# Reading the moving operand of every fp32r product as two interleaved streams, in a two-layer streaming encoder

## The chip, the core and the metric

The kernel runs on one core of one Trainium2 chip. The metric is device time in microseconds for one execution, from the first to the last instruction of the program with what lies around it. A program's time is the median of several executions; the profile is of one more execution, whose span is given beside it.

## The reference

The reference is a trunk of two layers on an input of 1024 frames by 1024 features, in float32. Every layer is `x = x + mixer(RMSNorm(x))`, and a final RMSNorm follows. Layer 0 projects the normalised input to 7168 columns, runs a diagonal complex state-space layer with a GLU on one part and retention over eight heads on another, multiplies each by its own SiLU gate and maps both back. Layer 1 is a gated convolution module. Cut to its matrix products:

```python
def mixer_ab(h, w_in, ...):
    proj = h @ w_in                                   # 1024 x 1024 by 1024 x 7168
    u_s5, g_s5, q, k, v, g_ret = jnp.split(proj, cuts, axis=-1)
    y_s5 = s5_mixer(u_s5, ...)                        # holds gelu(y) * sigmoid(y @ glu_w + glu_b)
    y_s5 = y_s5 * jax.nn.silu(g_s5)
    y_ret = retention(q, k, v) * jax.nn.silu(g_ret)
    return jnp.concatenate([y_s5, y_ret], axis=-1) @ w_out     # 2048 columns to 1024

def mixer_conv(h, w_in, conv_w, conv_b, ln_g, ln_b, w_out):
    a, b, g = jnp.split(h @ w_in, 3, axis=-1)         # 1024 x 1024 by 1024 x 3072
    u = a * jax.nn.sigmoid(b)
    u = causal_depthwise_conv(u, conv_w) + conv_b     # 31 taps
    u = jax.nn.silu(layernorm(u)) * jax.nn.silu(g)
    return u @ w_out                                  # 1024 x 1024 by 1024 x 1024
```

## The kernel before, in words

Activations lie with their features on the 128 partitions and the frames along the free dimension, so that a row block of 128 features by 1024 frames is worked on in two halves of 512 frames (`HALF`). A large matrix product is a loop over output row blocks `nb`, halves `h` and eight blocks `kb` of the contraction.

**How a float32 product is made of fp32r products.** Every float32 operand is split into a high part in the type fp32r and a low part, the rest, in fp32r as well (`xh`, `xl`, `wh`, `wl`). `mm3` (lines 175 to 183) then issues three products into the same PSUM bank: `wh` with `xh` (L181), `wh` with `xl` (L182) and `wl` with `xh` (L183). The weight block of 128 by 128 is stationary and 512 frames of the activations move through it. `gemm` calls `mm3` for eight blocks of the contraction, so one bank takes 24 products. In the value projection of retention the roles are turned: 128 frames are stationary and the weights move, 256 columns at a time in `ret_values` (L1091 to L1093) and 512 in `ret_values_wide` (L1114 to L1116). The last row blocks of the last projection (`mm_oc`) are taken in quarters of 256 frames.

These products are, by the program's names: `mm_u` 384, `mm_g` of layer 0 768, `mm_k` and `mm_q` 192 each, `mm_v` 192 of 512 columns and 384 of 256, `mm_glu` 336, `mm_wo` 768, `mm_b`, `mm_a` and `mm_g` of layer 1 384 each, and `mm_oc` 336 of 512 columns and 96 of 256. Together that is 4320 products of 512 columns and 480 of 256 columns. Everywhere the moving operand is a run of adjacent elements. Other products, of the state-space part and of the retention heads, have 128 columns or fewer in float32 and go through lines of their own (L848, L912, L918, L1170, L1204).

**How a bank is emptied.** The banks of these products rotate over three (`ps_mm`), so a bank is wanted again after two other row blocks. Each is read once by VectorE or ScalarE: `u_block` (L358) multiplies by the normalisation `R` and writes the frames in another order, reading bank and `R` at a step of eight elements; `gate_block` (L373), `project` (L1045), `w_out` (L1394), `ab` (L1445) and `w_out_c` (L1672) are VectorE operations on adjacent elements; `ret_values` (L1094, L1118), the tanh of `ab` (L1432) and the SiLU of `gates` (L1457) are ScalarE operations. The GLU forms its product as seven smaller products with sums between them; its partial sums `gu2` and `gu3` are kept in SBUF, and `gated` (L1314) takes the tanh of a finished sum.

**What sets the order.** Code is recorded in Python with priorities (`self.at`) and explicit constraints (`issue_after`), and a scheduler of the tile framework puts each engine's queue in order at build time. Weights come in through SyncE's DMA queue two blocks ahead (`wnext`), are rounded to the high part by ScalarE (L171, L148) and the low part is formed by VectorE or GpSimd (L172) or read back from HBM.

Of the kernel before, what the change touches and what calls it, by code (L numbers as in the profile page):

```python
# [14 lines left out]
AF = mybir.ActivationFunctionType  # L15
# [20 lines left out]
G0 = 3  # L36

# [15 lines left out]
class Trunk:  # L53
# [121 lines left out]
    def mm3(self, ps, w, kb, x, start, stop, more=False):  # L175

        nc = self.nc
        wh, wl = w
        xh, xl = x
        more = {"skip_group_check": True} if more else {}  # L180
        nc.tensor.matmul(ps, wh[:, kb, :], xh, start=start, stop=False, **more)  # L181
        nc.tensor.matmul(ps, wh[:, kb, :], xl, start=False, stop=False, **more)  # L182
        self.last_mm = nc.tensor.matmul(ps, wl[:, kb, :], xh, start=False, stop=stop, **more)  # L183
# [60 lines left out]
    def layer0_front(self, st):  # L244
# [106 lines left out]
        def u_block(nb):  # L351
            ut = uv.tile([P, 8, P], F32, name=f"ut_{nb}", tag="ut", bufs=2)

            def evac(h, ps):
                r = self.R[:, h * HALF:(h + 1) * HALF]

                with self.tc.issue_after(self.u_evac[0].ins) if nb == 1 else nullcontext():
                    self.u_evac[nb] = nc.vector.tensor_tensor(  # L358
                        ut[:, ::-1, h * 64:(h + 1) * 64], ps[:].rearrange("p (m j) -> p j m", j=8),
                        r.rearrange("p (m j) -> p j m", j=8), op=ALU.mult)  # L360
# [7 lines left out]
        def gate_block(nb, w, dst):  # L368
            gt = uv.tile([P, T], F32, name=f"gt_{nb}", tag="ut", bufs=2)

            def evac(h, ps):
                c = slice(h * HALF, (h + 1) * HALF)
                nc.vector.tensor_tensor(gt[:, c], ps[:], self.R[:, c], op=ALU.mult)  # L373
                nc.scalar.activation(gt[:, c], gt[:, c], AF.Silu)
# [653 lines left out]
    def ret_proj(self, pair):  # L1028
# [9 lines left out]
        def project(nm):  # L1038
            w = self.wnext(f"{nm}{pair}")
            raw = raws[nm] = self.rq.tile([P, T], F32, name=f"{nm}raw_{pair}", tag="raw", bufs=2)  # L1040
            for h in range(2):
# [3 lines left out]
                self.last_raw = nc.vector.tensor_tensor(raw[:, c], ps[:], self.R[:, c], op=ALU.mult)  # L1045
# [32 lines left out]
    def ret_values(self, pair):  # L1078
# [4 lines left out]
        for b in range(8):  # L1083
            ps = self.bank(f"mm_v{pair}_{b}", aux=False)
            h, o = b // 4, (b % 4) * P
            for kb in range(KB):
# [3 lines left out]
                wl = wv[i][1][:].rearrange("p (k a) n -> p k (a n)", a=2)[:, k4, :]  # L1090
                nc.tensor.matmul(ps[:, :256], xh[:, o:o + P], wh, start=kb == 0, stop=False)  # L1091
                nc.tensor.matmul(ps[:, :256], xh[:, o:o + P], wl, start=False, stop=False)
                nc.tensor.matmul(ps[:, :256], xl[:, o:o + P], wh, start=False, stop=kb == KB - 1)  # L1093
            self.last_v = nc.scalar.mul(vt[:, b, :], ps[:, :256], self.Rtok[:, b:b + 1])  # L1094
# [4 lines left out]
    def ret_values_wide(self):  # L1099
# [3 lines left out]
        for h in range(2):  # L1103
            vt = self.rp.tile([P, 4, HALF], F32, name=f"v_0_{h}", tag="v", bufs=2)
            pss = [self.bank(f"mm_v0_{h}_{b}") for b in range(4)]
            for j in range(4):
                wh, wl = (t[:].rearrange("p (k a) n -> p k (a n)", a=4)
                          for t in self.wnext(f"v0_{h}_{j}", 1 if h and j == 3 else 2))
                for b in range(4):
                    o = slice(b * P, (b + 1) * P)  # L1110
                    for k in range(2):
                        kb = 2 * j + k
                        xh, xl = self.xs[h][kb]
                        nc.tensor.matmul(pss[b][:], xh[:, o], wh[:, k, :], start=kb == 0, stop=False)  # L1114
                        nc.tensor.matmul(pss[b][:], xh[:, o], wl[:, k, :], start=False, stop=False)
                        nc.tensor.matmul(pss[b][:], xl[:, o], wh[:, k, :], start=False, stop=kb == KB - 1)  # L1116
            for b in range(4):
                last = nc.scalar.mul(vt[:, b, :], pss[b][:], self.Rtok[:, 4 * h + b:4 * h + b + 1])  # L1118
# [122 lines left out]
    def layer0_back_and_layer1(self, st):  # L1241
# [59 lines left out]
        def gated(nb, h, z):  # L1301
# [11 lines left out]
            with self.tc.issue_after(self.last_rs.ins) if h == nb == 0 else nullcontext():  # L1313
                nc.scalar.activation(z[:], src[:], AF.Tanh, scale=0.5, bias=hgb[:, nb:nb + 1])  # L1314
# [29 lines left out]
        for i, x in ((6, t2), (7, t3), (4, t4)):  # L1344
            for m in range(2):
# [18 lines left out]
        for m in range(2):  # L1364
            pss = [self.bank(f"mm_glu5{2 * m + a}", aux=False) for a in range(2)]
            for i, x in ((5, t1), (3, b22)):
                w = wn()
                for a in range(2):
                    n = 2 * m + a
                    product(pss[a], w, a, x, i == 3)  # L1370
                    if i == 5:
                        z = spare(f"mm_gluz{n}", n)
                        v.tensor_tensor(z[:], u3[n][:], pss[a][:], op=ALU.add)
                        gated(4 + n, 1, z)
# [9 lines left out]
        def w_out(h, nbs):  # L1384
            for nb in nbs:
# [8 lines left out]
                v.tensor_tensor(t[:], ps[:], xt[:], op=ALU.add)  # L1394
# [31 lines left out]
        def ab(h):  # L1426
            for nb in range(8):
# [4 lines left out]
                tanh = nc.scalar.activation(sg[:], pb[:], AF.Tanh, scale=0.5)  # L1432
# [12 lines left out]
                v.scalar_tensor_tensor(u[:, PADW:], sg[:], 1.0, pa[:], op0=ALU.add, op1=ALU.mult)  # L1445
# [4 lines left out]
        def gates(halves, nbs, hold={}):  # L1450
            for nb in nbs:
                wg = self.wnext(f"cg{nb}_{halves[0]}")
                for h in halves:
# [3 lines left out]
                    nc.scalar.activation(sg[:], pg[:], AF.Silu)  # L1457
# [196 lines left out]
        def w_out_c(h, nb, cols, hold=None):  # L1654
# [11 lines left out]
            def part(c):  # L1666
# [4 lines left out]
                with self.tc.issue_after(behind.ins) if behind else nullcontext():  # L1671
                    self.last_add = v.tensor_tensor(t[:, c], ps[:, :n], xt[:, c], op=ALU.add)  # L1672
# [230 lines left out]
```

## Time and profile before

| what | value |
|---|---|
| median of 3 runs | 1178.7 us (1178.5 to 1179.73) |
| the profiled execution, span | 1176.5 us, 17212 instructions |
| TensorE matmuls busy | 1168.5 us, 99% |
| TensorE weight loads busy | 979.8 us, 83% |
| VectorE busy | 844.5 us, 72% |
| ScalarE busy | 489.9 us, 42% |
| GpSimd busy | 655.3 us, 56% |
| mean granted TensorE clock | 0.999 |

The profile is that of one execution. In it PE is TensorE's matmul row, PEld its weight loads, DVE VectorE, ACT ScalarE, POOL GpSimd and SP SyncE. `L358` is line 358 of the kernel. Busy time of PE is not a measure of how full the array is, since matmuls overlap in a pipeline: the recorded duration of a matmul of 512 columns is 389 ns although the next one starts 227 ns later. What a product costs is therefore read from the distance of two starts.

### The profile page before, as it was taken

How to read it: one execution, taken by the hardware profiler on the slowest of the kernel's cores; microseconds unless marked ns; L12 is line 12 of the kernel's file. 1: busy time of each engine (PE TensorE's matmuls, PEld its weight loads, DVE VectorE, ACT ScalarE, POOL GpSimd, SP SyncE). 2: the span in 40 equal slices, each digit the busy share in tenths (PEclk: the TensorE clock that was granted, in tenths of full speed). 3: DMA queues.
4: the chain of work that ended last, by engine and by line, in shares of the span. 5: the costliest groups of instructions: out<-in, count | busy, mean ns of one | idle time of the engine just before them, and what ended most of it. 6: DMA issues, size and time to landing. Idle time of an engine off the chain costs nothing.

```text
span 1176.5 us, 17212 instructions
## 1 busy us (share of the span) xinstructions
PE 1168.5 (99%) x6286; PEld 979.8 (83%) x6286; DVE 844.5 (72%) x1464; ACT 489.9 (42%) x719; POOL 655.3 (56%) x448
## 2 busy tenths in 40 slices
PE   9999999999999999999999999999999999999997
PEld 8888888888888888989888888888888888888787
DVE  7975698777418359586679323599999899999834
ACT  6422223222223231333456324455535676344673
POOL 2059999888235444242673110588534567677663
PEclk9999999999999999999999999999999999999999
DMA  9344355555387666769998977665578654367765
GB/s 349 108 139 137 123 151 192 179 168 174 123 268 270 240 226 205 269 199 351 375 352 282 333 267 249 212 206 206 212 242 287 231 179 170 107 188 259 265 219 180
DMA packets 117637, 261.46 MB, mean 222 GB/s; under 512 B 10672, under 2 KB 42288, under 8 KB 116912
## 3 DMA queue, kind: packets, MB, share of 16 engines
q1 hardware_dynamic: 117552, 260.36, 65.5%
q8 instruction: 49, 0.80, 0.3%
q14 instruction: 36, 0.29, 0.1%
HBM read 181.48 MB, written 74.65 MB: 218 GB/s over the span
## 4 chain that ended last, share of the span: by engine, by line
PE 98%; issue 0%; ACT 0%; POOL 0%; DVE 0%; POOLq 0%; ACTq 0%
PE mm_g L181 8%; PE mm_g L182 7%; PE mm_g L183 7%; PE mm_wo L182 5%; PE mm_wo L183 5%; PE mm_wo L181 5%; PE mm_b L183 2%; PE mm_b L182 2%; PE mm_a L183 2%; PE mm_a L182 2%; PE mm_b L181 2%; PE mm_a L181 2%; PE mm_oc L183 2%; PE mm_u L182 2%; PE mm_oc L181 2%; PE mm_oc L182 2%
## 5 line engine op out<-in xcount | busy, mean ns | idle before, releaser
L1510 DVE SCALAR_TENSOR_TENSOR cv<-u,convw,cv 128x512 f32<-128x512 f32 x398 | 273.2, 751 | 11.0 <-ACT cv L1489 9.1
L1483 POOL TENSOR_TENSOR tp<-tp,tp 128x512 f32<-128x512 f32 x64 | 83.8, 1309 | 36.5 <-ACT tp L1482 35.5
L181 PE MATMUL mm_g<-xh,wh_g 128*128 128x512 f32 x256 | 101.8, 398 | 0.0
L183 PE MATMUL mm_g<-xh,wl_g 128*128 128x512 f32 x256 | 100.1, 391 | 0.0
L182 PE MATMUL mm_g<-xl,wh_g 128*128 128x512 f32 x256 | 100.0, 391 | 0.0
L417 POOL TENSOR_TENSOR s1q<-s1q,s1q 128x512 f32<-128x512 f32 x12 | 17.8, 1480 | 86.0 <-ACT s1q L412 86.0
L1482 ACT ACTIVATE tp<-u,convw 128x512 f32<-128x512 f32 x64 | 45.3, 718 | 34.2 <-POOL tp L1483 34.1
L181 PEld LDWEIGHTS mm_g<-xh,wh_g 128*128 128x128 f32 x256 | 48.0, 188 | 11.7 <-issue 1.2
L373 DVE TENSOR_TENSOR gt<-mm_g,R 128x512 f32<-128x512 f32 x32 | 21.9, 684 | 49.3 <-PE mm_g L183 49.3
L183 PEld LDWEIGHTS mm_g<-xh,wl_g 128*128 128x128 f32 x256 | 48.1, 188 | 10.4
L182 PEld LDWEIGHTS mm_g<-xl,wh_g 128*128 128x128 f32 x256 | 48.1, 188 | 9.9 <-issue 0.4
L172 POOL TENSOR_TENSOR wl_glu<-wf_glu,wh_glu 128x1024 fp32r<-128x1024 f32 x14 | 34.0, 2429 | 33.2 <-ACT wh_glu L171 27.4
L182 PE MATMUL mm_oc<-zl,wh_woc 128*128 128x512 f32 (+1 forms) x144 | 52.5, 365 | 0.0
L183 PE MATMUL mm_oc<-zh,wl_woc 128*128 128x512 f32 (+1 forms) x144 | 52.4, 366 | 0.0
L172 POOL TENSOR_TENSOR wl_v<-wf_v,wh_v 128x1024 fp32r<-128x1024 f32 x12 | 30.7, 2566 | 38.4 <-ACT wh_v L171 38.4
L181 PE MATMUL mm_oc<-zh,wh_woc 128*128 128x512 f32 (+1 forms) x144 | 52.1, 373 | 0.0
L181 PE MATMUL mm_wo<-ysh,wh_wos 128*128 128x512 f32 x128 | 50.2, 392 | 0.0
L181 PE MATMUL mm_g<-h1h,wh_cg 128*128 128x512 f32 x128 | 50.2, 392 | 0.0
L183 PE MATMUL mm_b<-h1h,wl_cb 128*128 128x512 f32 x128 | 49.9, 390 | 0.0
L181 PE MATMUL mm_b<-h1h,wh_cb 128*128 128x512 f32 x128 | 49.8, 389 | 0.0
L182 PE MATMUL mm_b<-h1l,wh_cb 128*128 128x512 f32 x128 | 49.8, 389 | 0.0
L182 PE MATMUL mm_wo<-ysl,wh_wos 128*128 128x512 f32 x128 | 49.8, 389 | 0.0
(526 smaller groups left out, 3650.7 us busy)
## 6 DMA issues: line engine op xcount, KB each, us to landing
wf_g<-w_ab SPq DMA_DIRECT2D x16, 512.0 KB
wf_wos<-w_out SPq DMA_DIRECT2D x16, 512.0 KB
wf_wor<-w_out SPq DMA_DIRECT2D x16, 512.0 KB
wf_cb<-w_c SPq DMA_DIRECT2D x16, 512.0 KB
wf_ca<-w_c SPq DMA_DIRECT2D x16, 512.0 KB
wf_woc<-w_out_c SPq DMA_DIRECT2D x16, 512.0 KB
wf_v<-w_v SPq DMA_DIRECT2D x12, 512.0 KB
wf_cg<-w_c SPq DMA_DIRECT2D x11, 512.0 KB
```

The lines of the kernel that those rows point to most:

```text
L172: self.low_made = lo[i].tensor_tensor(wl[:].rearrange(fl)[:, c], wf[:, c], h.bitcast(F32), op=ALU.subtract)
L181: nc.tensor.matmul(ps, wh[:, kb, :], xh, start=start, stop=False, **more)
L182: nc.tensor.matmul(ps, wh[:, kb, :], xl, start=False, stop=False, **more)
L183: self.last_mm = nc.tensor.matmul(ps, wl[:, kb, :], xh, start=False, stop=stop, **more)
L373: nc.vector.tensor_tensor(gt[:, c], ps[:], self.R[:, c], op=ALU.mult)
L417: nc.gpsimd.tensor_tensor(a, a, sq[:], op=ALU.add)
L1482: nc.scalar.mul(sk[:], u[:, k:k + HALF], cw[:, nb, k:k + 1])
L1483: gp.tensor_tensor(s0[:], s0[:], sk[:], op=ALU.add)
L1510: v.scalar_tensor_tensor(dst[:], *tap, accs_[i][:], op0=ALU.mult, op1=ALU.add)
```

## The change

The moving operand of each of the 4800 products is viewed with its columns in another order. The 512 columns are seen as two halves of 256, and the product takes a column of the first half, then one of the second: 0, 256, 1, 257 and so on (for 256 columns: 0, 128, 1, 129). The array writes its results to the bank in the order in which columns arrive, so the bank holds the frames interleaved. Each reader of a bank now reads it with a step of two elements, the even ones and then the odd ones, and writes them as two runs of adjacent elements, which restores the natural order. The stationary operand and its load stay as they are, and the same values are multiplied and summed.

In `u_block` the step in the bank goes from eight elements to sixteen, and `R` is still read at a step of eight. In the GLU the partial sums stay in the interleaved order of the banks, and only the last step (the tanh in `gated`, or the last sum for row blocks 4 to 7) restores the natural one. Because a bank can't be reordered in place, product 4 of the GLU now goes to a bank of the rotating three and its finished sum to a spare bank (`mm_gluy`), where before both were in the spare one.

No instruction is added, removed or moved by this: every engine's queue holds the same operations in the same order as before, apart from that name.

```diff
+LANES = 2
+def mv(ap):
+    return ap.rearrange("p (a c) -> p c a", a=LANES)
+def un(ap):
+    return ap.rearrange("p (c a) -> p a c", a=LANES)
+def nat(ap):
+    return ap.rearrange("p (a c) -> p a c", a=LANES)
...
@@ mm3
         xh, xl = x
+        xh, xl = mv(xh), mv(xl)
...
@@ u_block
+                o = ut[:, ::-1, h * 64:(h + 1) * 64].rearrange("p j (a m) -> p j a m", a=LANES)
...
-                        ut[:, ::-1, h * 64:(h + 1) * 64], ps[:].rearrange("p (m j) -> p j m", j=8),
-                        r.rearrange("p (m j) -> p j m", j=8), op=ALU.mult)
+                        o, ps[:].rearrange("p (m j a) -> p j a m", j=8, a=LANES),
+                        r.rearrange("p (a m j) -> p j a m", j=8, a=LANES), op=ALU.mult)
@@ gate_block (project, w_out and w_out_c alike)
-                nc.vector.tensor_tensor(gt[:, c], ps[:], self.R[:, c], op=ALU.mult)
+                nc.vector.tensor_tensor(nat(gt[:, c]), un(ps[:]), nat(self.R[:, c]), op=ALU.mult)
@@ ret_values (ret_values_wide alike)
+                wh, wl = mv(wh), mv(wl)
...
-            self.last_v = nc.scalar.mul(vt[:, b, :], ps[:, :256], self.Rtok[:, b:b + 1])
+            self.last_v = nc.scalar.mul(nat(vt[:, b, :]), un(ps[:, :256]), self.Rtok[:, b:b + 1])
@@ the GLU
-                nc.scalar.activation(z[:], src[:], AF.Tanh, scale=0.5, bias=hgb[:, nb:nb + 1])
+                nc.scalar.activation(*((z[:], src[:]) if turned else (nat(z[:]), un(src[:]))), AF.Tanh, scale=0.5,
+                                     bias=hgb[:, nb:nb + 1])
...
-                    ps = spare(f"mm_glu{i}{n}", n) if i == 4 else self.bank(f"mm_glu{i}{n}", aux=False)
+                    ps = self.bank(f"mm_glu{i}{n}", aux=False)
...
-                        v.tensor_tensor(ps[:], u3[n][:], ps[:], op=ALU.subtract)
-                        gated(4 + n, 0, ps)
+                        z = spare(f"mm_gluy{n}", n)
+                        v.tensor_tensor(nat(z[:]), un(u3[n][:]), un(ps[:]), op=ALU.subtract)
+                        gated(4 + n, 0, z, True)
@@ ab and gates
-                tanh = nc.scalar.activation(sg[:], pb[:], AF.Tanh, scale=0.5)
+                tanh = nc.scalar.activation(nat(sg[:]), un(pb[:]), AF.Tanh, scale=0.5)
...
-                v.scalar_tensor_tensor(u[:, PADW:], sg[:], 1.0, pa[:], op0=ALU.add, op1=ALU.mult)
+                v.scalar_tensor_tensor(nat(u[:, PADW:]), nat(sg[:]), 1.0, un(pa[:]), op0=ALU.add, op1=ALU.mult)
```

More of the change, by code (lines that the diff above doesn't have):

```diff
@@ L1044, in project @@
                 self.gemm(ps[:], w, self.xs[h])
[L1045 removed]
+                self.last_raw = nc.vector.tensor_tensor(nat(raw[:, c]), un(ps[:]), nat(self.R[:, c]), op=ALU.mult)
             return self.last_raw
@@ L1113, in ret_values_wide @@
                         xh, xl = self.xs[h][kb]
-                        nc.tensor.matmul(pss[b][:], xh[:, o], wh[:, k, :], start=kb == 0, stop=False)
-                        nc.tensor.matmul(pss[b][:], xh[:, o], wl[:, k, :], start=False, stop=False)
-                        nc.tensor.matmul(pss[b][:], xl[:, o], wh[:, k, :], start=False, stop=kb == KB - 1)
+                        wk, wj = mv(wh[:, k, :]), mv(wl[:, k, :])
+                        nc.tensor.matmul(pss[b][:], xh[:, o], wk, start=kb == 0, stop=False)
+                        nc.tensor.matmul(pss[b][:], xh[:, o], wj, start=False, stop=False)
+                        nc.tensor.matmul(pss[b][:], xl[:, o], wk, start=False, stop=kb == KB - 1)
             for b in range(4):
-                last = nc.scalar.mul(vt[:, b, :], pss[b][:], self.Rtok[:, 4 * h + b:4 * h + b + 1])
+                last = nc.scalar.mul(nat(vt[:, b, :]), un(pss[b][:]), self.Rtok[:, 4 * h + b:4 * h + b + 1])
             res.append(vt)
@@ L1299, in layer0_back_and_layer1, with gated @@
         held = []
-        def gated(nb, h, z):
+        def gated(nb, h, z, turned=False):
             yg = lp.tile([P, HALF], F32, name=f"yg{nb}_{h}", tag="u", bufs=5)
@@ L1372, in layer0_back_and_layer1 @@
                         z = spare(f"mm_gluz{n}", n)
-                        v.tensor_tensor(z[:], u3[n][:], pss[a][:], op=ALU.add)
-                        gated(4 + n, 1, z)
+                        v.tensor_tensor(nat(z[:]), un(u3[n][:]), un(pss[a][:]), op=ALU.add)
+                        gated(4 + n, 1, z, True)
                     else:
@@ L1393, in w_out @@
                 t = lp.tile([P, HALF], F32, name=f"x1_{nb}_{h}", tag="ev", bufs=3)
-                v.tensor_tensor(t[:], ps[:], xt[:], op=ALU.add)
+                v.tensor_tensor(nat(t[:]), un(ps[:]), nat(xt[:]), op=ALU.add)
                 nc.sync.dma_start(self.x1_d[rows(nb), hs(h)], t[:])
@@ L1456, in gates @@
                     sg = lp.tile([P, HALF], F32, name=f"sgg{nb}_{h}", tag="ev", bufs=3)
-                    nc.scalar.activation(sg[:], pg[:], AF.Silu)
+                    nc.scalar.activation(nat(sg[:]), un(pg[:]), AF.Silu)
                     nc.sync.dma_start(self.gs_d[rows(nb), hs(h)], sg[:])
@@ L1671, in part @@
                 with self.tc.issue_after(behind.ins) if behind else nullcontext():
-                    self.last_add = v.tensor_tensor(t[:, c], ps[:, :n], xt[:, c], op=ALU.add)
+                    self.last_add = v.tensor_tensor(nat(t[:, c]), un(ps[:, :n]), nat(xt[:, c]), op=ALU.add)
                 with self.tc.issue_after(self.halved.ins) if h == 0 and nb >= N0 else nullcontext():
```

## The prediction

> **What bounds the kernel now.** I read the head of the page first: its span, the busy times, the granted clock and the chain that ended last.
>
> ```profile
> span 1176.5 us, 17212 instructions
> PE 1168.5 (99%) x6286; PEld 979.8 (83%) x6286; DVE 844.5 (72%) x1464; ACT 489.9 (42%) x719; POOL 655.3 (56%) x448
> ...
> PEclk9999999999999999999999999999999999999999
> ...
> PE 98%; issue 0%; ACT 0%; POOL 0%; DVE 0%; POOLq 0%; ACTq 0%
> ```
>
> The chain lies on PE for 98% of the span at the full granted clock. A matmul's price goes into the time almost one to one, in either direction. PE hardly waits for anyone; this is its longest wait:
>
> ```profile
> PE idle L273 <- DVE mhalf L218: 1.1, 1, 1.1
> ```
>
> So the question is what one product costs. Recorded durations overlap, and I take the distance of starts from the timeline (start, duration). First a run of `mm_b`, 512 columns each, 14 rows in all:
>
> ```profile
> 800.03 0.39 PE L181 MATMUL mm_b<-h1h,wh_cb 128*128 128x512 f32 x1
> 800.26 0.39 PE L182 MATMUL mm_b<-h1l,wh_cb 128*128 128x512 f32 x1
> 800.49 0.39 PE L183 MATMUL mm_b<-h1h,wl_cb 128*128 128x512 f32 x1
> ...
> 802.98 0.39 PE L182 MATMUL mm_b<-h1l,wh_cb 128*128 128x512 f32 x1
> ```
>
> Thirteen distances in 2.95 us: 226.9 ns each. Then a run of `mm_v`, 256 columns each, 27 rows in all:
>
> ```profile
> 469.94 0.28 PE L1091 MATMUL mm_v<-wh_v,xh 128*128 128x256 f32 x1
> 470.06 0.28 PE L1092 MATMUL mm_v<-wl_v,xh 128*128 128x256 f32 x1
> ...
> 473.06 0.28 PE L1093 MATMUL mm_v<-wh_v,xl 128*128 128x256 f32 x1
> ```
>
> Twenty-six distances in 3.12 us: 120.0 ns each. The difference, 106.9 ns for 256 columns, is 0.418 ns a column, and what is left of 120.0 ns is 13.1 ns a product, whatever its length. So a product has two parts that the change could touch: columns (4320 x 512 + 480 x 256 = 2.335 million, 976 us) and starts (4800 x 13.1 ns = 62.9 us). Together they are 1039 us of the span of 1176.5 us; the rest belongs to products that the change leaves alone and to gaps. The span is 2.2 us under the median of the runs; I make the sum against the span and add 2.2 us.
>
> **The change part by part.** No instruction is added or moved, so no queue is longer and no wait is new. Two things change their duration: 4800 reads of the moving operand, and the operations that empty the banks.
>
> *The moving read.* Before, four adjacent columns lie in 16 bytes. After, each column lies 1024 bytes from the one before it (512 for 256 columns), and the place next to it is read one column later. No product of before reads its moving operand in steps, so the price is bounded by other engines' rows, operations of one size with and without steps:
>
> ```profile
> L373 DVE TENSOR_TENSOR gt<-mm_g,R 128x512 f32<-128x512 f32 x32 | 21.9, 684 | 49.3 <-PE mm_g L183 49.3
> L358 DVE TENSOR_TENSOR ut<-mm_u,R 128x512 f32<-128x512 f32 x16 | 17.9, 1134 | 11.9 <-PE mm_u L183 11.8
> L1713 DVE TENSOR_TENSOR fo<-x,rf_R 128x256 f32<-128x256 f32 x12 | 4.3, 416 | 2.1 <-PE rf_R L485 1.6 <-ACT RF L1703 0.4
> L1237 ACT CAST zh<-co 128x512 fp32r<-128x512 f32 x11 | 6.8, 620 | 8.5 <-POOL co L1643 8.4
> L148 ACT CAST wh_wor<-wf_wor 128x1024 fp32r<-128x1024 f32 x8 | 8.4, 1055 | 20.2 <-PE mm_wo L182 18.7 <-PE mm_b L182 1.5
> L759 ACT COPY hq<-s_bbr 128x512 f32<-128x512 f32 x1 | 1.1, 1107 | 5.5 <-POOL s_bbr L563 5.5
> L938 ACT ACTIVATE yn<-yp 128x1024 f32<-128x1024 f32 x8 | 16.7, 2088 | 18.4 <-DMA yp<-y_d 13.2 <-issue 5.2
> L265 ACT ACTIVATE sq<-x 128x1024 f32<-128x1024 f32 x7 | 7.4, 1057 | 5.7 <-DVE ss L268 5.4
> ```
>
> On VectorE an adjacent element costs (684 - 416) / 256 = 1.05 ns. L358 reads bank and `R` in steps of 32 bytes and takes 1134 - 684 = 450 ns more for 512 elements, 0.88 ns each: 1.84 times the adjacent price. On ScalarE an adjacent element costs (1055 - 620) / 512 = 0.85 ns. L759 reads SBUF in steps of 64 bytes and pays (1107 - 620) / 512 = 0.95 ns more, 2.1 times. L938 reads in steps of 512 bytes and comes back to the neighbouring place after eight elements, the nearest thing to the change's pattern; it pays (2088 - 1057) / 1024 = 1.01 ns more, 2.2 times. (Its function is another than L265's, so a little of that may be the function.) Both engines that leave a short run at each element take about twice as long, and coming back soon doesn't help L938.
>
> The Trainium skill has a rule for this (*SBUF — State Buffer*, the note on cachelines under *Door 1: The DMA port swizzle*): SBUF is organised in lines of 16 bytes, and an access pays unless at least two accesses fall on a line. The ScalarE rows agree with it, 2.1 and 2.2 times; no row here shows it for TensorE. It speaks against this change, where no two accesses in a row fall on one line; with two accesses' time for each column, an estimate by it is the same 976 us.
>
> I take the doubling, 0.418 ns more a column. The lower bound is nothing, since the read may be served at any address at the same pace. The upper bound takes the penalty in nanoseconds and not in cycles, 0.88 to 1.01 ns a column. A gain isn't excluded either, but I look for it only in the 13.1 ns of the start, since no row has a cheaper column. The value is taken from the ratio because both engines' extra time is about one of their own element periods, which differ (0.85 and 1.05 ns).
>
> *Emptying the banks.* The reads of step two lie between L373 (684 ns, adjacent) and L358 (1134 ns, a step of eight): 0 to 450 ns each, on ScalarE up to about the same. A gain is excluded, as the number of elements stays. Step two leaves two values within 16 bytes, which puts it nearer to L373; I take 0. L358 itself keeps a step beyond that and I take 0 there too. The cover: a bank is wanted again two row blocks later, 2 x 24 x 226.9 ns = 10.9 us, against 1.1 us. What would be exposed is VectorE's own time where it is nearly full:
>
> ```profile
> 720.00:900.00 180.00, 180.00 (x792) 148.34 (x792) 151.49 (x224) 86.55 (x124) 104.77 (x73) 1.00 0.65 223
> 900.00:1080.00 180.00, 180.00 (x803) 149.06 (x802) 168.03 (x259) 103.49 (x154) 117.98 (x85) 1.00 0.58 191
> ```
>
> (The third busy time is VectorE's.) In the second stretch it has 12 us left, and `mm_a` gives it eight such reads there (the third busy time again):
>
> ```profile
> 900.00:1080.00 180.00, 46.51 (x192) 36.04 (x192) 5.46 (x8) 1.00 0.58 191
> ```
>
> 8 x 0.45 = 3.6 us at worst: it stays below PE. Elsewhere VectorE waits for the banks, not the reverse:
>
> ```profile
> DVE gt L373 <- PE mm_g L183: 49.3, 14, 4.8
> DVE x L1394 <- PE mm_wo L183: 43.6, 13, 13.5
> ```
>
> *The GLU's bank.* Product 4 moves from the spare banks to the three rotating ones; with 12 products, 2.7 us, between uses and one read each, I take 0.
>
> *The sum.* 2.335 million columns x 0.418 ns = 976 us more on PE, all on the path. 1176.5 + 976 = 2152.5 us, and with 2.2 us **2155 us**. With the ratio of VectorE (1.84) it is 820 us more, 1999 us; with that of L938 (2.19) 1161 us more, 2340 us. No other engine comes near the bound then, since PE's stretches all double.
>
> **The rivals.**
>
> *The starts get cheaper (faster).* The 13.1 ns may be the wait for the first data of the moving read, exposed because the stream then takes data as fast as it comes; two streams might overlap such waits. One row speaks for a read-side cost. The float32 products of the state-space part appear as two records each, 16 for a group:
>
> ```profile
> 140.33 1.95 PE L912 MATMUL y<-U,W 128*128 128x128 f32 x16
> L912 PE MATMUL y<-U,W 128*128 128x128 f32 x128 | 15.6, 275 | 0.0
> ```
>
> (1.95 - 0.275) / 15 = 111.7 ns a record. If each of its 128 columns takes two steps of the array (an estimate from the column price above), 107.0 ns are columns and 4.7 ns start: products that take fresh data at half the pace start more cheaply. If the interleaved read brought 13.1 down to 4.7 ns, 4800 x 8.4 = 40 us go and the time is **1138 us**; if all 13.1 ns went, 62.9 us, 1116 us. It decides from 0.5 ns a product (2.4 us), if the columns keep their price. Against it: the column order doesn't change the pace at which data is wanted, and the start may belong to changing the weights. PE's gain would also shrink in the stretch from 900 to 1080 us: 803 x 8.4 ns takes PE to 173.3 us there, with VectorE at 168.0 to 171.6 us. The Trainium skill (*TensorE: Matmul & The Clock Gate*, *Wait — 56ns, not 53.3ns?*) gives a start-to-start of the columns plus about 2.5 ns; 226.9 ns here doesn't agree with it, and with its 2.5 ns an estimate of this rival would be about 1128 us.
>
> *The order is free (no change).* If TensorE is fed at the same pace at any address, 226.9 ns stay, the reads of the banks stay hidden, and the time is **1179 us**. For it: no row shows TensorE slowed by where its data lie. Against it: two engines that read the same memories do pay, and every product of before reads adjacent columns, so that nothing could show it. The Trainium skill says on the page *TensorE: Matmul & The Clock Gate* (*Step-by-step: what each phase is for*) that throughput is one column a cycle; the 0.418 ns agree, but all rows are of adjacent columns.
>
> *The penalty is a time, not a cycle.* With 0.88 to 1.01 ns a column the change costs 2055 to 2358 us: about **3230 to 3540 us**. The extra times of the two engines lie within 15% of each other, which speaks for it; that four columns of 0.418 ns come out of 16 bytes in 1.67 ns without a stall doesn't contradict it.
>
> *VectorE becomes the bound (slightly slower).* With products as before and 450 ns on each bank read it would need 12 us in the stretch from 900 to 1080 us and gets 3.6; only from 1.5 us a read does it decide. At most some 4 us, **1183 us**.
>
> **How the numbers follow.** The doubling 0.38; a penalty between nothing and 1999 us 0.04; the penalty as a time 0.12; VectorE's bound 0.03; no change 0.13; cheaper starts 0.30, since the 13.1 ns are real and nothing in the trace says whose they are. What a measurement of this kernel tells from no change is about 0.2%, 2.4 us. Slower is 0.38 + 0.04 + 0.12 + 0.03 = 0.57, the same 0.13, faster 0.30. The likeliest case's own range is 1999 to 2340 us. As cases of both signs hold the chance, the range runs from 1115 us, all starts gone, to 2340 us; it leaves out the penalty as a time and the tails.
>
> **What would show it.** In the profile after, the distance of two starts of `mm_b` decides: 0.44 us for the forecast, 0.90 us for the penalty as a time, 0.227 us for no change, 0.22 us or less for cheaper starts; and `mm_v` beside it, whose distance tells columns from starts (0.227 us if columns doubled, 0.112 us if starts fell to 4.7 ns). The weight loads should keep their duration. L373 between 684 and 1134 ns gives the price of step two. The forecast is wrong if `mm_b` keeps its distance, whatever the total does.

## The result and the profile after

| | before | after |
|---|---|---|
| median of the runs | 1179.0 us (1178.5 to 1179.7, 4 runs) | 1146.1 us (1142.8 to 1147.6, 4 runs) |
| the profiled execution | 1178.7 us, span 1176.5 us | 1147.6 us, span 1145.8 us |

The ratio of after to before is 0.9717, with a 95% interval of 0.9699 to 0.9734. The kernel is 33 us faster; the forecast was 2155 us, and the rival *The starts get cheaper* (1116 to 1138 us) named the right side.

First the head of the page after, with the shares of the chain that ended last:

```profile
span 1145.8 us, 17197 instructions
PE 1123.9 (98%) x6286; PEld 983.4 (86%) x6286; DVE 853.5 (74%) x1464; ACT 488.2 (43%) x719; POOL 657.7 (57%) x448
...
PE 34%; DVE 8%; DMA 7%; issue 2%; POOL 2%; ACT 1%; SPq 1%; POOLq 0%; ACTq 0%; DVEq 0%
```

PE is busy for 44.6 us less than before (1168.5), but its idle time has grown from 8.0 to 21.9 us. The chain that ended last can be followed back only to 510 us, so its shares add up to about 55% of the span: PE has 34 of these 55, where before it had 98% of the whole span, and VectorE, transfers, GpSimd and ScalarE hold most of the rest. Something was won on PE, and part of it went into waits.

What was won shows in the distance of starts, the row that the prediction called decisive. A run of `mm_b` on the timeline after (start, duration), 14 rows in all:

```profile
780.00 0.38 PE L200 MATMUL mm_b<-h1h,wh_cb 128*128 128x512 f32 x1
...
782.81 0.38 PE L201 MATMUL mm_b<-h1l,wh_cb 128*128 128x512 f32 x1
```

Thirteen distances in 2.81 us are 216 ns each, where 226.9 ns stood before. A run of `mm_v` with 256 columns, 30 rows in all:

```profile
463.73 0.28 PE L1114 MATMUL mm_v<-wh_v,xl 128*128 128x256 f32 x1
...
466.97 0.28 PE L1113 MATMUL mm_v<-wl_v,xh 128*128 128x256 f32 x1
```

Twenty-nine distances in 3.24 us are 111.7 ns each, where 120.0 stood. So a start became 10.7 to 11.1 ns cheaper at 512 columns (the surveys below give 215.8 ns) and 8.3 ns at 256: 4320 x 11 + 480 x 8.3 is about 51 us. Only 30.7 us of it are in the span of the profiled execution. The longest waits of PE show where some of the other 20 us are (what PE waited for, us in total, times, longest):

```profile
PE rt L1249 <- DVE mv L1236: 2.9, 1, 2.9
PE cst L509 <- DVE cs L1616: 2.7, 1, 2.7
PE mm_v L1137 <- POOL wl_v L190: 2.3, 1, 2.3
PE mm_glu L200 <- DVE mm_gluz L1397: 1.9, 1, 1.9
```

Before, the longest was 1.1 us. The second part is the clock. Windows around the waits of `mm_v` and of `cst` (PE busy, PEld, DVE, ACT, POOL, then the granted clock):

```profile
350.00:360.90 10.90, 8.58 (x40) 7.02 (x38) 9.06 (x7) 2.29 (x4) 8.91 (x5) 1.00 0.90 294
360.90:364.30 3.40, 3.40 (x10) 2.64 (x9) 3.40 (x2) 1.36 (x2) 3.40 (x2) 0.51 0.52 208
...
1067.00:1074.30 7.30, 4.61 (x21) 3.72 (x21) 6.98 (x11) 3.45 (x5) 4.45 (x3) 1.00 0.62 231
1074.30:1077.70 3.40, 3.40 (x5) 1.30 (x4) 1.53 (x4) 2.81 (x5) 2.74 (x2) 0.50 0.96 348
```

In the first line PE is idle for 2.3 of 10.9 us; in the second it is busy throughout, but at half the clock. Three such stretches of 3.4 us stand in the clock records of after, from 360.9, 459.9 and 1074.3 us on; before has none until the last 4.2 us. Each costs up to 1.7 us. The account of the 51 us: 30.7 out, 13.9 in more idle time, up to 5.1 at half clock, about 1 left over.

The reads of the banks cost nothing more. The groups of after that answer to L373 and L358 of before, and ScalarE's reader of `mm_b` (busy, mean ns):

```profile
L393 DVE TENSOR_TENSOR gt<-mm_g,R 128x512 f32<-128x512 f32 x32 | 21.8, 681 | 29.5 <-PE mm_g L202 29.5
L378 DVE TENSOR_TENSOR ut<-mm_u,R 128x512 f32<-128x512 f32 x16 | 17.2, 1089 | 9.4 <-PE mm_u L202 9.4
...
L1456 ACT ACTIVATE sb<-mm_b 128x512 f32<-128x512 f32 x16 | 9.4, 588 | 0.0
```

681 ns against 684, 1089 against 1134, and ScalarE's 588 ns are 588 before:

```profile
L1432 ACT ACTIVATE sb<-mm_b 128x512 f32<-128x512 f32 x16 | 9.4, 588 | 0.0
```

A step of two in a bank cost these readers nothing.

### The profile page after: what moved, and what is told of

Its sections match the earlier page's. It is cut to its first block, busy times and chain, and to the rows that moved or that the text cites. A ratio compares the mean times of both kernels' runs of the same rounds, so it can differ in the third digit from the quotient of the medians.

```text
span 1145.8 us, 17197 instructions
## 1 busy us (share of the span) xinstructions
PE 1123.9 (98%) x6286; PEld 983.4 (86%) x6286; DVE 853.5 (74%) x1464; ACT 488.2 (43%) x719; POOL 657.7 (57%) x448
## 4 chain that ended last, share of the span: by engine, by line
PE 34%; DVE 8%; DMA 7%; issue 2%; POOL 2%; ACT 1%; SPq 1%; POOLq 0%; ACTq 0%; DVEq 0%
DVE cv L1534 5%; PE mm_wo L202 5%; PE mm_wo L201 5%; PE mm_wo L200 5%; PE mm_b L201 2%; PE mm_b L202 2%; PE mm_b L200 2%; PE mm_a L202 2%; PE mm_a L201 2%; PE mm_a L200 2%; PE mm_oc L202 2%; PE mm_oc L201 1%; PE mm_oc L200 1%; DMA wf_glu<-w_glu 1%; DMA t_d<-th 1%
## 5 line engine op out<-in xcount | busy, mean ns | idle before, releaser
L200 PE MATMUL mm_g<-xh,wh_g 128*128 128x512 f32 x256 | 98.9, 386 | 0.0
L201 PE MATMUL mm_g<-xl,wh_g 128*128 128x512 f32 x256 | 97.3, 380 | 0.0
L202 PE MATMUL mm_g<-xh,wl_g 128*128 128x512 f32 x256 | 97.2, 380 | 0.0
L201 PE MATMUL mm_u<-xl,wh_u 128*128 128x512 f32 x128 | 48.4, 381 | 0.7 <-DVE xl L316 0.7
L202 PE MATMUL mm_wo<-ysh,wl_wos 128*128 128x512 f32 x128 | 48.5, 379 | 0.0
```

## The experiments

Two questions: why is a start cheaper, and where do the 20 us go that PE freed and the kernel did not get?

### The two halves of the change alone

One kernel has the readers' steps of two, but products that read one stream; its columns land in the wrong order.

```diff
 def mv(ap):
-    return ap.rearrange("p (a c) -> p c a", a=LANES)
+    return ap
```

> The products read adjacent columns as before, and the banks are read with the step of two as in the change (the values come out in another order than the reference's). It measures the price of the reads alone. Theory that the readers cost nothing (their operations last as long as before and were hidden): 1177 to 1181 us, the time before. Rival, that the readers take some of the gain: 1183 us or more.

It took 1178.8 us, a ratio of 1.0004 (0.9995 to 1.0013). The other has the products' two streams and readers of adjacent columns, so that its columns are misplaced too.

```diff
 def un(ap):
-    return ap.rearrange("p (c a) -> p a c", a=LANES)
+    return ap.rearrange("p (a c) -> p a c", a=LANES)
...
@@ u_block
-                        o, ps[:].rearrange("p (m j a) -> p j a m", j=8, a=LANES),
+                        o, ps[:].rearrange("p (a m j) -> p j a m", j=8, a=LANES),
```

> The products read two streams as in the change, and the banks are read in adjacent order as before (the frames stay in the interleaved order, so the values are not the reference's). Theory that the products bring all of the gain: 1142 to 1148 us, as the change. Rival, that the readers give part of it back: 1135 to 1140 us.

It took 1146.1 us, 0.9730 (0.9708 to 0.9751). The products bring the whole gain and the readers cost nothing.

### Ways of reading, the first survey

The kernel's own work is left out; for each way of reading, 48 products stand back to back, with the same stationary operands in turn. (In the excerpt `x` is the viewed moving operand and `wk` the stationary one.) The names: `two` is the change's order, `four`, `eight` and `many` are 4, 8 and 64 streams; `inline` takes columns 0, 2, 1, 3, `nextline` 0, 4, 1, 5, `pairs` 0, 1, 256, 257.

```diff
+VIEWS = {
+    "adj": lambda x: x,
+    "two": lambda x: x.rearrange("p (a c) -> p c a", a=2),
...
+    "eight": lambda x: x.rearrange("p (a c) -> p c a", a=8),
...
+    "steptwo": lambda x: x.rearrange("p (c a) -> p a c", a=2),
...
+                for i in range(24):
+                    wk = w[i % KB] if isinstance(w, list) else w[:k, 0 if same else i % KB, :m]
+                    nc.tensor.matmul(bank[:m, :n], wk, x[:k] if k < P else x, start=i == 0, stop=i == 23)
```

> A kernel of its own that leaves the whole reference out: it runs 48 fp32r products of 512 columns (or 256) for each of some views of the moving operand, with the same data, and writes the input as its output. The distance of two starts is read for each view. Measured so far: 226.9 ns for adjacent columns, about 216 ns for two streams. Theory of place (the start is dear when successive columns come out of the same 16 bytes, whatever the pattern's form): a pattern that reorders columns only within 16 bytes (inline: 0, 2, 1, 3) stays at 227 ns; neighbouring groups of four taken in turn (nextline: 0, 4, 1, 5), two, four and eight far streams and a step of two fall to 216 ns. Theory of form (a pattern with a second dimension starts sooner, whatever it reads): inline falls to 216 ns too, and so do 32 runs of 16 adjacent columns (runs). Theory of the weights (the start is the change of the weights, or their load disturbs the moving read): with adjacent columns a stationary operand of 64 or 32 columns, or the same one each time, cuts 227 ns to 220 ns or less. The forecast's penalty for leaving a line should still show somewhere if it exists: 430 ns for 64 streams (many) or a step of eight (stepeight); if TensorE has no such penalty they stay at 216 to 227 ns. bf16 columns: 216 ns in any order if the start is fp32r's alone.

The timeline gives a row for each view. The start of a row taken from the start of the next, divided by 48, is the distance of two products:

```profile
19.39 11.04 PE L61 MATMUL adj<-xr,wr 128*128 128x512 f32 x48
30.27 10.52 PE L61 MATMUL two<-xr,wr 128*128 128x512 f32 x48
40.63 13.75 PE L61 MATMUL four<-xr,wr 128*128 128x512 f32 x48
54.21 23.56 PE L61 MATMUL eight<-xr,wr 128*128 128x512 f32 x48
77.57 20.90 PE L61 MATMUL many<-xr,wr 128*128 128x512 f32 x48
98.27 21.85 PE L61 MATMUL steptwo<-xr,wr 128*128 128x512 f32 x48
...
140.64 11.08 PE L61 MATMUL inline<-xr,wr 128*128 128x512 f32 x48
151.55 10.52 PE L61 MATMUL nextline<-xr,wr 128*128 128x512 f32 x48
161.91 16.16 PE L61 MATMUL pairs<-xr,wr 128*128 128x512 f32 x48
...
266.04 11.08 PE L61 MATMUL same<-xr,wr 128*128 128x512 f32 x48
276.96 11.36 PE L61 MATMUL wstep<-xr,wr 128*128 128x512 f32 x48
```

(30.27 - 19.39) / 48 = 226.7 ns for one stream, 215.8 for two, 282.9 for four, 486.7 for eight, 431.3 for 64, and 452 for every second column (its next row starts at 119.94). No theory that names place, form or weights alone survives these rows. With the same stationary operand each time (`same`) the distance is still 227.5 ns. With stationary operands of 64 and 32 columns it is 230.2 and 231.9 ns ((244.56 - 233.51) / 48 and (266.04 - 254.91) / 48), although their loads are recorded at 134 and 109 ns in place of 188. So the start is not the price of a change of the weights nor of a longer load; a load stands before every product in all these rows. `inline` and `nextline` have views of the same form, and cost 227.3 and 215.8 ns. `nextline` swaps between places 16 bytes apart and costs what `two` costs at 1024 bytes, so the distance of the streams is nothing either. And eight streams pay 487 ns, a little more than the 0.44 us that the forecast had for two.

From these rows I formed another theory, **lanes**: the columns of the moving operand come in alternately through two lanes, the even and the odd ones, and what counts is how many accesses in a row of one lane lie in the same 16 bytes. Two streams give four to each lane: 216 ns. One stream gives two: 227. Every second column, eight streams or 64 give one: 431 to 487. It was made after the fact, and four streams (283) and pairs (333) lie between.

### Eight streams in the whole kernel

```diff
-LANES = 2
+LANES = 8
```

> The change with eight streams in place of two; the readers of the banks then take a step of eight. Theory of place and theory of form: 216 ns a product as with two streams; the readers cost up to 450 ns more each on VectorE, partly exposed where it is nearly full: 1146 to 1165 us. The forecast's line penalty, if it begins beyond two streams: 430 ns a product, over 2000 us.

It took 2349.9 us, 1.9939 times before (1.9905 to 1.9972), and the first rows of its `mm_b` are 0.49 us apart:

```profile
1606.57 0.69 PE L200 MATMUL mm_b<-h1h,wh_cb 128*128 128x512 f32 x1
1607.06 0.69 PE L201 MATMUL mm_b<-h1l,wh_cb 128*128 128x512 f32 x1
```

The penalty that I forecast exists and costs what the forecast's upper ratio said (2.19 times, 2340 us). Two streams are not in its reach.

### The second survey, which the lane theory had to foretell

> The kernel's own work is left out: 48 products per way of reading, and the mean distance of starts is read from the trace. Theory of lanes (formed after the first survey): even and odd columns of the moving operand come through two lanes, and a start costs 13 ns, 2.5 ns or much more by how many accesses of one lane in a row fall in the same 16 bytes. It expects two streams 216 ns, two streams of every second place (twostep) 227 to 251 ns (two accesses a lane in 16 bytes), of every fourth place (twoquad) about 430 ns (one access), two streams with groups of four taken backwards 216 to 222 ns, pairs 333 ns, octets 227 to 251 ns; each column read twice in a row 216 ns; two streams from column 1 216 to 219 ns; streams 255 columns apart (510 columns) 215 ns; and with shorter products, 384, 320, 192, 128 columns, 11 ns less for two streams than for one at each length until another limit holds both. Rival, that adjacency alone costs (two columns in a row out of the same 16 bytes): each column read twice takes 227 ns or more, octets and one stream the same 227 ns, and twostep 216 ns as two. Rival, that steps inside a stream cost by their bytes: twostep equals a stream of every second place, 451 ns. bf16: pairs from two places 216 ns if it is read in pairs, 484 ns as two streams otherwise.

The same kernel with other views:

```diff
+    "twostep": lambda x: x.rearrange("p (a c s) -> p s c a", a=2, s=2),
+    "twoquad": lambda x: x.rearrange("p (a c s) -> p s c a", a=2, s=4),
...
+        run("twice", wr, xr[:, :256].unsqueeze(2).broadcast_to([P, 256, 2]), HALF)
...
+        for n, nm in ((384, "tqadj"), (320, "fradj"), (192, "thadj"), (128, "sadj")): ...
```

The rows that decide, on the timeline again:

```profile
20.08 11.04 PE L57 MATMUL adj<-xr,wr 128*128 128x512 f32 x48
30.96 10.52 PE L57 MATMUL two<-xr,wr 128*128 128x512 f32 x48
41.32 11.08 PE L57 MATMUL twostep<-xr,wr 128*128 128x512 f32 x48
52.23 21.91 PE L57 MATMUL twoquad<-xr,wr 128*128 128x512 f32 x48
73.97 10.54 PE L57 MATMUL twoback<-xr,wr 128*128 128x512 f32 x48
...
134.01 10.53 PE L57 MATMUL twice<-xr,wr 128*128 128x512 f32 x48
144.37 10.52 PE L57 MATMUL fourtimes<-xr,wr 128*128 128x512 f32 x48
...
216.50 5.50 PE L57 MATMUL thadj<-xr,wr 128*128 128x192 f32 x48
221.84 5.51 PE L57 MATMUL thtwo<-xr,wr 128*128 128x192 f32 x48
227.19 5.50 PE L57 MATMUL sadj<-xr,wr 128*128 128x128 f32 x48
232.53 5.52 PE L57 MATMUL stwo<-xr,wr 128*128 128x128 f32 x48
237.89 41.42 PE L57 MATMUL plain<-xf,wf 128*128 128x512 f32 x96
279.14 52.00 PE L57 MATMUL plaintwo<-xf,wf 128*128 128x512 f32 x96
330.47 11.58 PE L57 MATMUL adj<-xr,wr 128*128 128x512 f32 x48
```

`twostep`, two accesses of a lane in 16 bytes, takes 227.3 ns; steps in a stream by their bytes would have made it 451. `twoquad`, one access, takes 453 (about 430 expected). `twoback` 216.3, `octets` 243.5, each column read twice 215.8, where adjacency as the cost asked for 227. Streams 255 columns apart take 215.4 ns, and two streams from column 1 take 216.5. For fp32r the theory foretold every class, though not the 237 ns of one stream from column 1. It is a way of counting that these rows follow; that there are two lanes is not shown. Outside fp32r it failed: bf16 in pairs from two places takes 266 ns and not 216, bf16 as two streams 484 (first survey) against 216 adjacent, and plain float32 gets slower, (330.47 - 279.14) / 48 = 1069 ns a product as two streams against 859.

By length, the difference of the two ways is 10.8 ns at 384 columns (173.3 and 162.5) and 10.9 at 320 (146.7 and 135.8), as at 512: it does not grow with the columns, so it is a time per product and no price per column. At 192 and at 128 columns all four rows stand at 111.3 to 111.7 ns. Another limit holds short products there, whichever way they are read; what it is, these rows don't say.

### Whose the start is

> The kernel's own work is left out: products alone, 48 per view, distances read from the trace. What is asked: whose is the start, and is it a wait for the first data of a read? Theory of slack: a lane that gets two accesses out of 16 bytes is fetched exactly as fast as the array takes columns, so the next product's first data come late by a fixed 11 ns; with four accesses in 16 bytes the fetch is ahead and the next start is hidden; with one the fetch is at half the pace and each column costs double. It expects a constant of about 13 ns for one stream at 480 and 448 columns (213 and 200 ns), 2.5 to 3 ns for two streams (203 and 190 ns), and for a stream of every second place a price by column, 0.83 to 0.88 ns (about 422 ns at 480, 394 at 448, 338 at 384, 225 at 256, 113 at 128). Where one-stream and two-stream products alternate, one of the two distances is 227 and the other 216 ns, a mean of 221 ns; by slack the product behind a one-stream product starts late, so the distance from one to two is 227 and from two to one 216. Rival: the start belongs to the product's own read, whatever went ahead, and the two distances lie the other way round; or the start is paid at every change of the view, and both are 227 ns or more. Plain float32: the short products of the state-space part stand at about 111 ns for 128 columns and not at half of 256's, if a floor other than the columns holds them.

```diff
+                nm = (first, second)[i % 2]
+                nc.tensor.matmul(bank[:], wr[:, i % KB], VIEWS[nm](xs), start=i == 0, stop=i == 47)
```

Where products of one stream and of two alternate, the starts from an even product (one stream) on stand at

```profile
44.44 0.61 PE L67 MATMUL mix_adj_two<-xr,wr 128*128 128x512 f32 x2
44.67 0.61 PE L67 MATMUL mix_adj_two<-xr,wr 128*128 128x512 f32 x2
44.88 0.61 PE L67 MATMUL mix_adj_two<-xr,wr 128*128 128x512 f32 x2
```

0.23 us from one to two, 0.21 from two to one (means over the run 231.8 and 215.0 ns). The late time lies behind the product that reads one stream, which is what slack expected: a one-stream product leaves the fetch no lead, and the next one's first columns come late. That the late time lies inside the one-stream product would look the same; the rows tell only that it belongs to that product. Where two streams alternate with every second column, the means are 234.6 ns from two streams on and 434.6 ns back, against 215.8 and 451.5 for each alone: some 19 ns of that price stand ahead of the dearer product's own start, which slack as stated does not foresee. For every second column the price is by column, as expected (425 ns at 480 columns, 340 at 384). At 480 and 448 columns one stream takes 216.7 and 203.1 ns, 3 ns more than expected, and two streams 202.5 and 189.2 ns, as expected. So the difference is 14 ns at these two lengths and 11 at 512, 384 and 320; why is open. Plain float32 takes 215.8 ns a record at 256 columns and 111.6 at 128, which is not half: the limit on short products holds there too, as expected.

### Where 20 us went: single waits

Three kernels move work off the engines that PE now waits for: the low parts of the wide value weights from GpSimd to VectorE, one more tap of the convolution's second half from VectorE to ScalarE and GpSimd, and both.

```diff
-LO_V = {f"g{i}" for i in range(1, 10)} | {"u4", "u5", "u6", "wos", "wor"}
+LO_V = {"v0"} | {f"g{i}" for i in range(1, 10)} | {"u4", "u5", "u6", "wos", "wor"}
...
-    TAPS = (5, 5)
+    TAPS = (5, 6)
```

> The changed kernel, with the low parts of the weights of the wide value product made on VectorE instead of GpSimd. If part of what the cheaper starts free is given back at the wait of mm_v for GpSimd (2.3 us and the half clock behind it, about 1.7 us more), the time falls by 2 to 4 us against the changed kernel, to 1142 to 1144 us, that wait is gone from the list, and the half clock after 360 us too. Rival: the next wait takes its place (VectorE later for the convolution in the same stretch), and the time stays at 1146 us or rises by 1 to 3 us.

> The changed kernel, with one more tap of the convolution's second half taken from VectorE and given to ScalarE and GpSimd. If the stretch from 900 us on is now held by VectorE (168.7 of 180 us busy, PE 177.3), the wait of cst for VectorE (2.7 us) and the half clock behind it go, and the time falls by 2 to 5 us to 1141 to 1144 us. Rival: GpSimd becomes the last in the convolution and the wait only changes its name: 1146 us or slower.

> The changed kernel with both moves, low parts on VectorE and one more tap away from it. If the two waits are separate, the gains add: 4 to 8 us, 1138 to 1142 us. If a wait only changes its name, 1145 us or more.

They took 1143.4 us (0.9696, 0.9677 to 0.9715), 1147.6 us (0.9736, 0.9723 to 0.9749) and 1144.7 us (0.9724, 0.9700 to 0.9747). The first has the lowest median of all runs and lies where its theory wanted it (1142 to 1144 us), but its interval overlaps that of the change (0.9699 to 0.9734), so none of the three is told apart from the change. Both moves together came out between the sum (1138 to 1142 us) and the rival's 1145 us. The waits say why. With the low parts on VectorE, PE's longest waits are:

```profile
PE ro L1221 <- DVE sc L1198: 3.2, 1, 3.2
PE cst L509 <- DVE cs L1616: 2.7, 1, 2.7
```

The wait of `mm_v` is gone, and one of `ro` (retention's readout, for VectorE) stands in its place. The half clock after 360 us is gone as well, and again there are three such stretches, from 488.5, 604.5 and 1072.1 us on. With one more tap, `cst` waits 2.0 us instead of 2.7, and `cm` waits 1.3 us for GpSimd. With both, `cst` waits 0.7 us, `ro` 2.5 and `cm` 1.6. In each a wait changes its name, as the rival had it.

### Where 20 us went: the helpers' load

Two kernels, the change and before, make no low parts of the weights and read the high parts in their place (so the result lacks the low parts); this takes GpSimd from 658 to 465 us and VectorE from 854 to 773.

```diff
-        wl = self.wp.tile([P, KB, P], F32R, name=f"wl_{name}", tag="wl", bufs=3)
-        yield wh, wl
+        yield wh, wh
...
-            nc.scalar.copy(h, wf[:, c])
-            self.low_made = lo[i].tensor_tensor(wl[:].rearrange(fl)[:, c], wf[:, c], h.bitcast(F32), op=ALU.subtract)
+            self.low_made = nc.scalar.copy(h, wf[:, c])
```

> The changed kernel with less work for GpSimd and VectorE: the low parts of the weights are not made, and the products that read them read the high parts instead (the two halves of an fp32 weight are no longer separate; the count and shape of the products stay). Theory: some 20 of the 51 us freed on TensorE were given back because VectorE and GpSimd no longer keep up; with less for them to do most of the new waits go, and the time is 1125 to 1135 us, 4320 x 10.9 + 480 x 8.4 = 51 us under the same edit of the kernel before, give or take 6 us. Rival: the waits stand in chains of small steps (norms, gates, decays) whose length no lighter load shortens, or in transfers, and the time stays at 1140 us or more, 31 to 36 us under the same edit of the kernel before.

> The kernel before with the same edit (no low parts made, the high parts read in their place). TensorE bounds it at 1168.5 of 1176.5 us, so both theories expect little: 1170 to 1179 us. It is the yardstick for the same edit of the changed kernel: a difference of 47 to 55 us between the two by the theory that the helpers gave back the rest, 31 to 36 us by the rival.

The changed kernel took 1145.5 us with the edit, as without it; the theory wanted 1125 to 1135. Two waits of about 3 us are left there, and the clock halves again behind the first, for 6.8 us from 484.8 us on:

```profile
PE ro L1219 <- DVE sc L1196: 3.0, 1, 3.0
PE cst L507 <- DVE cs L1614: 2.9, 1, 2.9
```

The yardstick was not as still as both theories thought: before took 1185.9 us with the edit, 1.0054 of before (1.0038 to 1.0069), with less work for GpSimd and VectorE. In its profiled run PE is idle for 12.5 us, where it was 8.0. The edit does more than lighten the load: the scheduler puts the queues in another order, the same way in both kernels. Against the order without the edit, 94 of PE's products, 55 of VectorE's operations and 66 of ScalarE's stand elsewhere in their queues. How much of the 0.5% comes of that is not shown. The difference of the two, 40 us, lies between the theories' bounds. So less load on GpSimd and VectorE, with the queues in this order, does not bring the 20 us out.

The last kernel leaves four of VectorE's 26 taps per row block out of the convolution's second half.

```diff
-            for k in range(NT[h], CONV_K):
+            for k in range(NT[h] + 4 * h, CONV_K):
```

> The changed kernel with four of the 26 taps that VectorE adds for each of the eight row blocks of the convolution's second half left out (those taps are missing from the output): 8 x 4 x 0.753 = 24 us less for VectorE, nothing else touched. Theory: from 900 us on the changed kernel stands on VectorE (168.7 of 180 us busy, PE 177.3, the wait of cst for cs 2.7 us and 3.4 us of half clock behind it). Then the wait of cst is gone, PE is busy 179 of 180 us there, and the time is 1140 to 1143 us, 3 to 6 us under the changed kernel's 1146. Rival: cst waits for the chain of small steps at the convolution's end whatever the load, its wait stays at 2 to 3 us, and the time is 1145 to 1147 us.

Its runs took 1140.3 to 1152.3 us, median 1145.0 (0.9730, 0.9706 to 0.9753). The longest wait of the profiled one:

```profile
PE mm_oc L200 <- DVE x L1696: 3.4, 1, 3.4
```

`cst`'s wait is gone from the list, as the theory said, and PE is busy 176.6 of 180 us from 900 us on, not 179. But the edit touched more than VectorE's load, which the expectation overlooked. These are the `cst` products in the change and in this kernel (durations, first and last start):

```profile
L509 PE MATMUL cst<-cs,ones x2: 940/1000/1061, 1074.0 to 1074.7; 128*128 128x512 f32 x2
L509 PE MATMUL cst<-cs,ones x2: 592/592/592, 1047.2 to 1047.6; 128*128 128x512 f32 x2
```

In the change they stand behind 126 products of `mm_oc` in PE's queue, in this kernel behind 44: the scheduler has moved them. So it is not shown whether the lighter load or the new place ended the wait. Its end brought 1 us at most in the median (1145.0 against 1146.1), and the longest wait is now that of `mm_oc` for VectorE's sums `x`, up to 1074.0 us, where `cst` started in the change.

What holds after these six: the 20 us stand in many waits of up to 3.4 us, mostly for VectorE's short steps between two stages, and where one went, another stood in its place. What each wait hangs on is not shown, since of the six edits only the one of the low parts of the wide value weights left PE's queue in its order. Which order of work would bring all of the 20 us out was not found. One more thing hides differences here: the runs of a kernel that has the change lie 0.2% (the extra tap) to 1.0% (fewer taps) apart, where those of the kernel before lie 0.1 to 0.3% apart, so a few us between two profiled executions mean little.

## Why the prediction was wrong

**What bounds the kernel: right.** The chain on PE at 98% meant that a product's price goes into the time, and the eight streams show it at full length: 4320 x (487 - 227) + 480 x (224 - 120) is 1173 us (224 ns from its `mm_v`), and 1171 came out. "In either direction" went too far: downwards, only 33 of the 51 us on PE came out.

**"I take the doubling": the step that failed.** The doubling was read from VectorE's and ScalarE's rows, and for TensorE it is real at eight streams, 2.15 times, and for every second column, 1.99. It failed in what I took to be the same pattern. The row that I called the nearest (L938) comes back to the neighbouring place after eight elements; the change comes back after two. On TensorE itself these are 486.7 and 215.8 ns. "Coming back soon doesn't help L938" was said of eight and used for two. The Trainium skill's rule (*SBUF — State Buffer*, the note on cachelines: at least two accesses on a line) I counted over all columns in a row, where two streams have one; counted for the even and the odd columns apart, one stream has two and two streams have four, and then the fp32r rows above follow it in their order, though it has no place for a gain beyond two accesses.

**"A gain isn't excluded, but I look for it only in the start": right.** The columns kept their price, (226.7 - 146.7) / 192 = 0.4167 ns for one stream and (215.8 - 135.8) / 192 = 0.4167 for two, from 320 to 512 columns, and the start went from 13.4 to 2.5 ns (226.7 and 215.8 ns less 512 columns at 0.4167 ns). The Trainium skill's figure (*TensorE: Matmul & The Clock Gate*, *Wait — 56ns, not 53.3ns?*) holds for two streams, 215.8 ns, and not for fp32r in one, 226.9.

**The rival's size, 4.7 ns: right by chance for 256 columns, wrong as a start.** The 111.7 ns of the state-space records are no start: at 128 and 192 columns fp32r products stand at 111 to 112 ns however they are read. Before's own trace could have told it, since records of only 64 columns stand 112 ns apart there (median of 15 distances):

```profile
L446 PE MATMUL ss<-ones,ssum x16: 275/275/305, 35.4 to 37.1; 128*128 128x64 f32 x16
```

A limit of the same size ends the gain of the 256-column products at 111.7 ns, where 2.5 ns of start would have allowed 109.2; that it is the same one is not shown.

**Emptying the banks at nothing: right** (681 against 684 ns; 1.0004 for the readers alone). **The GLU's bank at nothing: not shown to cost.** No moved bank is among the longest waits; the 1.9 us of `mm_glu` are for VectorE's sum `mm_gluz`, which stood in a spare bank before too, and the readers alone, which keep the moved bank, took 1.0004.

**The cover on VectorE: seen, and too narrowly.** From 900 to 1080 us the prediction had VectorE near PE once the starts fell, and there `cst` waits 2.7 us. These are the windows of after (the third busy time is VectorE's):

```profile
400.00:560.00 160.00, 156.88 (x1187) 143.63 (x1185) 120.31 (x318) 49.01 (x66) 59.90 (x36) 0.99 0.75 251
...
900.00:1080.00 180.00, 177.31 (x817) 153.22 (x816) 168.71 (x261) 102.69 (x151) 129.50 (x91) 0.99 0.62 205
```

But PE also loses 3 us from 400 to 560 us, where VectorE is busy for 120 of 160 us. The rival's 1138 us took all 40 us as gain; busy shares don't show which short chain becomes late when PE gets 4% faster.

**The chances.** The row that could have told the rival from the forecast, TensorE's own price for a step, was not in the trace, and I gave the nearest other engine the larger chance.

## What to carry to other kernels

A penalty of another engine says that a pattern can cost, not that this one does: where the moving operand is fp32r, count the accesses per 16 bytes separately for the even and the odd columns, and let a survey of 48 products price a second stream. Keep it to fp32r: here bf16 and plain float32 got slower as two streams. When a bound engine gets 4% faster, expect less: of 51 us here 33 came out, and the rest went into short waits for engines that no busy share marks as full, and into the half clock behind some of these waits. And when work is taken out to test a wait, compare the order of the queues before and after: here the scheduler moved the product that waited.

## What the runs showed of the hardware

- A moving operand of fp32r in 512 columns costs 226.7 ns as one stream, 215.8 as two, 282.9 as four and 486.7 as eight; the first difference is 11 ns at 320, 384 and 512 columns and 14 at 448 and 480, and products of 128 and 192 columns stand at 111 to 112 ns.
- In the changed kernel the half-clock stretches after waits last 3.4 us and begin on a grid: 459.9 - 360.9 = 99.0 us is 29 times 3.413, and 1074.3 - 459.9 = 614.4 us is 180 times. The Trainium skill (*TensorE: Matmul & The Clock Gate*, Part 1) has a free-running window of 3413 ns, and the trace agrees; it asks for an idle window, where here less was enough. Laid on this grid, in the profiles of the seven kernels with two streams, half clock followed all ten windows in which PE was idle for 1.88 us or more and none with 1.72 us or less (idle time counted from the starts and durations of the matmuls); of the six windows between, it followed two. So the same wait can cost 1.7 us more or nothing, by where it falls: with both moves (low parts and tap) `ro` waits 2.5 us, at most 1.4 us of PE's idle time lie in one window, and the clock stays at 1.00.
- Half clock came without a wait too: in the first survey it lasts from 324.4 us to the end, in a row of bf16 products that read every eighth column, with PE recorded busy for 40.64 of the 41.50 us from 324.5 us on.
- Reading the stationary operand at a step of two costs the product 6 ns, against 227.5 for `same`: (288.16 - 276.96) / 48 = 233.3 ns, where 288.16 us is the start of the row behind `wstep` in the first survey.
